# A hybrid decoder layer in float32 on one core: sums over partitions in the products' row pattern, a bias table written by Pool, and the first half's down product in plain products of 320 columns

## The chip, the cores and the metric

The kernel runs on 1 core of one Trainium2 chip, in one launch. The metric is the device time of that core in microseconds (us). The kernel before took 1602.73 us as the median of 3 runs (1602.7 to 1602.85).

## The reference

One decoder layer is computed in float32 for 320 tokens: a prompt of 256 and 8 samples of 8. The model width D is 2048.

```python
xn = rms_norm(x, g_mix)
z = xn @ w_in                      # B | C | h | q | k | v | gate_conv | gate_attn
u = c_gate * h_conv                # short causal convolution of width 3
y_conv = (b_gate * conv_out) @ w_conv_out
bias = rel_bias[t5_bucket(dist)]   # 32 buckets x 16 heads, window 128
attn = softmax_with_sink(q k^T / 8 + bias) v
y_attn = attn @ w_attn_out
h = x + (sigmoid(gate_c) * y_conv + sigmoid(gate_a) * y_attn) @ w_o
hn = rms_norm(h, g_ffn)
h = h + (silu(hn @ w_gate) * (hn @ w_up)) @ w_down     # 5632 hidden features
y = rms_norm(h, g_final)
```

Beside y, the new window of keys and values and the last rows of u are returned.

## The kernel before, in words

**Products.** Features lie on the partitions and the 320 tokens along the free axis. A float32 product is made of three products of rounded parts (type fp32r): with w = whi + wlo and x = xh + xl it is whi x xh + whi x xl + wlo x xh, all added up in PSUM. The weights are the stationary operand, 128x128 at a time, and the 320 tokens stream past. Each weight tile comes by DMA on SP's queue (wraw, 512 KB), ACT rounds it to whi (L128) and DVE subtracts to get wlo (L129); four wraw and three whi/wlo buffers let this run ahead of TensorE. `product` (L161 to L184) does one group: 2 blocks of 128 outputs, 96 products where the depth is 2048.

**Row pattern.** The 320 tokens of a chunk are stored as 5 pieces of 64 (`fives`), a fixed pitch apart, and are streamed 4 tokens of each piece in turn (`turns`), so the moving operand has the shape 16x5x4. In the built programs each such row starts 64 bytes past a multiple of 256; the leads LEAD_X, LEAD_C, LEAD_A and LEAD_M set that. A few products don't follow the pattern: the sums over partitions for the norms (`over_partitions`, L198, with a 128x128 tile of ones as weights, ones_r), the transposes and products of the attention, and a `nudge` (L194), which multiplies a plain row and throws the result away. There are four nudges.

**Order.** The stages follow one another on TensorE: kv, q, three kinds of gates and inputs (C, H, B, four rounds), the gates of the merge with the two output products (gc, ga, yc, ya, eight rounds), wo, and the feed-forward part. Attention is a generator (`side_work`) that is advanced one step after each weight tile of a running product, so its small products stand between those of q, C, H and B. A scheduler in the framework orders each engine's instructions from these; dependencies alone make an engine wait.

**First norm** (`first_norm`, L428). The squares are added up in xacc, split into two parts (`two_parts`, L186), and summed over the partitions in `prb`, between the second and the third of the four weight tiles of the first q product. Just ahead of it two small products (`pe_`, L441) multiply the bias table, 32 buckets x 16 heads, by a one-hot matrix of 32 x 128; DVE copies the result into e_sb, and Pool's queue stores it (e_scr) and loads the rows of the bias from there for the scores.

**Feed-forward part.** The 44 chunks of hidden features are done in two halves of 28 and 16. In each half, gate (fg) and up (fu) products come first, two chunks at a time, then the down product. Between the first fg and fu stands the second norm's sum (`pss`). **The down product** (`down`, L938) goes by blocks of 512 outputs with four accumulators. A chunk's hidden row holds both parts of the later 192 tokens, but only the rounded part of the first 128. So per chunk there are four products of 512 columns with whi (L962), one of 512 columns with the row's low part as weights and whi streaming (L966, into dl, or into rowacc for the last block), and four of 320 columns with wlo (L970). The low parts come out with tokens on the partitions; they are kept in ylow and added at the end. The second half's last block is taken apart and written out by hand (L1114 to L1161), and adds to the same rowacc.

Of the kernel before, what the change touches and what calls it, by code (L numbers as in the profile page):

```python
# [21 lines left out]
WIN = 128  # L22
# [29 lines left out]
def hybrid_layer(ctx: ExitStack, tc: tile.TileContext, a: dict, o: list):  # L52
# [133 lines left out]
    def two_parts(src, tags=("ta", "tb")):  # L186

        n = src.shape[-1]
        hi, lo = (wk.tile([P, UL], F32R, tag=t, name=u("part"))[:, :n] for t in tags)
        nc.scalar.activation(hi, src, AF.Copy)  # L190
        nc.vector.tensor_sub(lo, src, hi.bitcast(F32))
        return hi, lo
# [5 lines left out]
    def over_partitions(out, parts):  # L198
        for i, x in enumerate(parts):
            nc.tensor.matmul(out, ones_r, x, start=i == 0, stop=i == 1)  # L200
# [70 lines left out]
    rel = zz.tile([NBK, NH], F32, name="rel")  # L271
    oh = zz.tile([NBK, WIN], F32, name="oh")
    rel_r = zz.tile([NBK, 2, NH], F32R, name="rel_r")
    oh_r = zz.tile([NBK, WIN], F32R, name="oh_r")
# [103 lines left out]
    def small_loads():  # L378

        behind = nc.gpsimd.tensor_copy(gate, xh(7)[:, 0, 0:1].bitcast(F32))  # L380
        with after(behind):
            nc.gpsimd.dma_start(rel, a["rel_bias"])
            nc.gpsimd.dma_start(oh, a["c_onehot"])
            nc.gpsimd.dma_start(sink_bc, sk[0].partition_broadcast(P))
            nc.gpsimd.dma_start(sink_s, bass.AP(sk.tensor, sk.offset, [[1, NH], [0, TS], [1, 1]]))
            nc.gpsimd.dma_start(st_sb, a["state_t"])
            nc.gpsimd.dma_start(blk, a["c_block"])
# [40 lines left out]
    def first_norm():  # L428
# [5 lines left out]
        parts = two_parts(xacc)  # L434
        nc.vector.tensor_copy(oh_r, oh)
        nc.scalar.activation(rel_r[:, 0], rel, AF.Copy)
        nc.vector.tensor_sub(rel_r[:, 1], rel, rel_r[:, 0].bitcast(F32))
        yield
        prb, pe_ = ps_aux("prb"), ps_aux("pe_")
        for i in range(2):  # L440
            nc.tensor.matmul(pe_[:NH, :WIN], rel_r[:, i], oh_r, start=i == 0, stop=i == 1)  # L441
# [7 lines left out]
        nc.vector.tensor_copy(e_sb[:, WIN - 1:2 * WIN - 1], pe_[:NH, :WIN])  # L449
# [481 lines left out]

    def parts_of(row):
        return placed(row[:, 0:P]), placed(row[:, P:])
# [4 lines left out]
    def down(half, c0):  # L938

        nf, f0 = FH[half], half * FH[0]  # L940
        ps = [ps_acc(u("dn")) for _ in range(4)]
        low = ps_aux(u("dl")) if c0 < E0 else rowacc
        sets = [[k] for k in range(0, nf, 2)]
        sets[-2:] = [sets[-2] + sets[-1]]
        for i, k0s in enumerate(sets):
            parts = {}
            for k0 in k0s:
                raw = wp.tile([P, 2, 512], F32, tag="wraw", name=u("wraw"), bufs=4)
                nc.sync.dma_start(raw, w_d[c0 // 512, :, f0 + k0:f0 + k0 + 2, :])
                hi = wp.tile([P, 2, 512], F32R, tag="whi", name=u("whi"), bufs=3)  # L950
                lo = wp.tile([P, 2, 512], F32R, tag="wlo", name=u("wlo"), bufs=3)
                split_to(hi, lo, raw)
                for j in range(2):
                    parts[k0 + j] = (hi[:, j, :], lo[:, j, :])
            end = i == len(sets) - 1
            order = [(k, c) for k in parts for c in range(4)]
            if end or i == 0:
                order.sort(key=lambda kc: kc[1])
            for k, c, m in passes(order, end):
                cs = slice(c * P, (c + 1) * P)  # L960
                if m == 0:
                    nc.tensor.matmul(  # L962
                        turns(placed(ps[c])), parts[k][0][:, cs], turns(a_move(k)), start=k == 0, stop=False
                    )
                elif m == 1 and c == 0:
                    nc.tensor.matmul(  # L966
                        low, a_low(k), parts[k][0], start=k == 0, stop=k == nf - 1 and c0 < E0
                    )
# [15 lines left out]
        if c0 < E0:  # L984
            ys = ylow[:, c0:c0 + 512]
            if half == 0:
                nc.scalar.activation(ys, low, AF.Copy)
            else:
                nc.vector.tensor_add(ys, low, ys)

    for half in range(2):
# [3 lines left out]
        a_move, a_low, a_first, free = a_rows(half)  # L995
        for fpair in range(nf // 2):
            c0 = (f0 + fpair * 2) * P
            if half == 0 and fpair == 1:
                nudge(hh, hl, P)
# [16 lines left out]
            if half == 1 and fpair == 0:  # L1016
                nudge(hh, hl, P)
# [4 lines left out]
            for c in range(2):  # L1022
                nc.vector.tensor_mul(gs[c], psu[c][:, :T], gs[c])
                f = fpair * 2 + c
                (first, rest), row = parts_of(gs[c]), a_move(f)
# [4 lines left out]
                if half == 1:  # L1030
                    nc.scalar.activation(a_first(f), gs[c][:, 0:P], AF.Copy)
# [46 lines left out]
        for c0 in range(0, D if half == 0 else E0, 512):  # L1078
            down(half, c0)
            if half == 1:  # L1080
# [183 lines left out]
```

## Time and profile before

| what | value |
|---|---|
| median of 3 runs | 1602.73 us (1602.7 to 1602.85) |
| profiled execution, span from first to last instruction | 1600.6 us; no other time is given for it |
| TensorE busy | 1592.1 us, 10957 products |
| DVE, ACT, Pool busy | 885.6, 651.4, 78.3 us |
| granted TensorE clock, mean | 0.999 |
| data moved | 258.14 MB, 161 GB/s over the span |

The chain of waits is the work that ended last, followed back from the last instruction; shown in order of time, a line gives the start (us), the duration (us) up to what follows, the engine, the tile written, the line of the program, and the count. A timeline of one engine has the same columns, then the tiles (out<-in) and their sizes, and in brackets the idle time ahead and what ended it. In a list of DMA issues the columns are the size in KB and the time from issue to landing. Products overlap, so the duration of a single one (302 ns for 320 columns) is longer than the step from one to the next.

### The profile page before, as it was taken

The numbers are of one execution on the slowest core, as the hardware profiler recorded it, in microseconds if no ns is written. First come the engines' busy times: TensorE is split into PE (matmuls) and PEld (weight loads), VectorE is DVE, ScalarE is ACT, GpSimd is POOL, SyncE is SP. The second block draws the span as 40 slices with busy tenths as digits, with TensorE's granted clock in tenths as the row PEclk, the third lists the DMA queues.
The fourth block names the chain that finished last, engine by engine and source line by source line (L and its number), as shares of the span: only waits on it lengthen the run. The fifth ranks groups of instructions, "written<-read, shape, count | busy, mean of one in ns | idle before, by whom it ended". The sixth has DMA issues, their size and how long they took to land.

```text
span 1600.6 us, 26409 instructions
## 1 busy us (share of the span) xinstructions
PE 1592.1 (99%) x10957; PEld 1555.5 (97%) x10957; DVE 885.6 (55%) x1316; ACT 651.4 (41%) x928; POOL 78.3 (5%) x123
## 2 busy tenths in 40 slices
PE   9999999999999999999999999999999999999998
PEld 9999999999999999999999999998888999999887
DVE  7879565444455555556555555553444455555556
ACT  7555433433333334444333333333333334344443
POOL 1101311000000003320000000000000000000000
PEclk9999999999999999999999999999999999999999
DMA  7554546545444545544444445455555544545552
GB/s 276 174 170 137 182 145 200 167 158 156 154 157 157 157 157 159 158 158 155 154 157 156 157 157 159 158 158 158 155 154 155 157 156 158 158 158 157 182 175 93
DMA packets 74400, 258.14 MB, mean 161 GB/s; under 512 B 8552, under 2 KB 11928, under 8 KB 74152
## 3 DMA queue, kind: packets, MB, share of 16 engines
q1 hardware_dynamic: 71880, 249.86, 49.4%
q0 software_dynamic: 1968, 5.90, 1.3%
q8 instruction: 86, 1.41, 0.4%
q10 hardware_dynamic: 432, 0.69, 0.1%
q14 instruction: 34, 0.28, 0.1%
HBM read 253.30 MB, written 5.08 MB: 161 GB/s over the span
## 4 chain that ended last, share of the span: by engine, by line
PE 99%; DVE 0%; ACT 0%; DVEq 0%; issue 0%
PE fu L175 18%; PE fg L175 18%; PE dn L962 9%; PE gc L175 7%; PE ga L175 7%; PE wo L175 7%; PE dn L970 6%; PE B L175 3%; PE C L175 3%; PE H L175 3%; PE q L175 3%; PE yc L175 3%; PE ya L175 3%; PE dl L966 2%; PE kv L366 2%; PE dn L1114 1%
## 5 line engine op out<-in xcount | busy, mean ns | idle before, releaser
L129 DVE TENSOR_TENSOR wlo<-wraw,whi 128x1024 fp32r<-128x1024 f32 (+1 forms) x460 | 561.7, 1221 | 588.7 <-ACT whi L128 580.5
L128 ACT ACTIVATE whi<-wraw 128x1024 fp32r<-128x1024 f32 (+1 forms) x460 | 485.0, 1056 | 717.3 <-PE dn L962 144.7
L962 PE MATMUL dn<-a_t,whi 128*128 128x512 f32 x640 | 211.1, 385 | 0.0
L175 PE MATMUL fu<-hh_t,whi 128*128 128x320 f32 x704 | 205.3, 302 | 0.0
L175 PE MATMUL fg<-hl_t,whi 128*128 128x320 f32 x704 | 205.3, 302 | 0.0
L175 PE MATMUL fu<-hl_t,whi 128*128 128x320 f32 x704 | 205.3, 302 | 0.0
L175 PE MATMUL fg<-hh_t,whi 128*128 128x320 f32 x704 | 205.3, 302 | 0.0
L175 PE MATMUL fg<-hh_t,wlo 128*128 128x320 f32 x704 | 159.0, 302 | 0.0
L175 PE MATMUL fu<-hh_t,wlo 128*128 128x320 f32 x704 | 159.0, 302 | 0.0
L970 PE MATMUL dn<-a_t,wlo 128*128 128x320 f32 x640 | 146.8, 302 | 0.0
L962 PEld LDWEIGHTS dn<-a_t,whi 128*128 128x128 f32 x640 | 118.8, 188 | 19.3
L175 PEld LDWEIGHTS fg<-hh_t,whi 128*128 128x128 f32 x704 | 131.9, 187 | 0.0
L175 PEld LDWEIGHTS fu<-hh_t,whi 128*128 128x128 f32 x704 | 131.9, 187 | 0.0
L175 PEld LDWEIGHTS fg<-hl_t,whi 128*128 128x128 f32 x704 | 131.8, 187 | 0.0
L175 PEld LDWEIGHTS fu<-hl_t,whi 128*128 128x128 f32 x704 | 131.8, 187 | 0.0
L970 PEld LDWEIGHTS dn<-a_t,wlo 128*128 128x128 f32 x640 | 111.2, 188 | 9.3
L175 PEld LDWEIGHTS fu<-hh_t,wlo 128*128 128x128 f32 x704 | 116.3, 187 | 0.0
L175 PEld LDWEIGHTS fg<-hh_t,wlo 128*128 128x128 f32 x704 | 116.3, 187 | 0.0
L175 PE MATMUL ga<-xl_t,whi 128*128 128x320 f32 x256 | 74.6, 301 | 0.0
L175 PE MATMUL gc<-xl_t,whi 128*128 128x320 f32 x256 | 74.6, 302 | 0.0
L175 PE MATMUL wo<-m_l,whi 128*128 128x320 f32 x256 | 74.6, 302 | 0.0
L175 PE MATMUL gc<-xh_t,whi 128*128 128x320 f32 x256 | 74.6, 301 | 0.0
(313 smaller groups left out, 2681.4 us busy)
## 6 DMA issues: line engine op xcount, KB each, us to landing
wraw<-in_w_in_dram SPq DMA_DIRECT2D x128, 512.0 KB, 3.8
wraw<-in_w_gate_dram SPq DMA_DIRECT2D x88, 512.0 KB, 3.8
wraw<-in_w_up_dram SPq DMA_DIRECT2D x88, 512.0 KB, 3.7
wraw<-in_w_down_dram SPq DMA_DIRECT2D x88, 512.0 KB, 3.6
wraw<-in_w_o_dram SPq DMA_DIRECT2D x32, 512.0 KB, 3.7
wraw<-in_w_conv_out_dram SPq DMA_DIRECT2D x16, 512.0 KB, 3.6
wraw<-in_w_attn_out_dram SPq DMA_DIRECT2D x16, 512.0 KB, 3.6
wraw<-in_w_kv_dram SPq DMA_DIRECT2D x6, 512.0 KB, 7.4
```

Of the source, the lines that this page charges most:

```text
L128: last["hi"] = nc.scalar.activation(hi, src, AF.Copy)
L129: last["lo"] = nc.vector.tensor_sub(lo, src, hi.bitcast(F32))
L175: last["mm"] = nc.tensor.matmul(turns(fives(ps[c][:, :T])), w[:, k, c * P:(c + 1) * P], turns(x(kc)), start=(kc == 0 and i == 0), stop=(kc ...
L366: last["mm"] = nc.tensor.matmul(turns(fives(ps[c][:, :T])), w[:, k, c * P:(c + 1) * P], turns(x(kc)), start=(kc == 0 and m == 0), stop=(kc ...
L962: nc.tensor.matmul(turns(placed(ps[c])), parts[k][0][:, cs], turns(a_move(k)), start=k == 0, stop=False)
L966: nc.tensor.matmul(low, a_low(k), parts[k][0], start=k == 0, stop=k == nf - 1 and c0 < E0)
L970: last["mm"] = nc.tensor.matmul(turns(placed(ps[c])[:, :, 0:JT]), parts[k][1][:, cs], turns(a_move(k)[:, :, 0:JT]), start=False, stop=k == ...
L1114: nc.tensor.matmul(turns(placed(ps[c])[:, :, JR:]), held[k][0][:, cs], turns(a_move(k)[:, :, JR:]), start=k == 0, stop=k == nf - 1,)
```

## The change

There are three edits, and what follows from them.

1. The norms' sums over partitions. `two_parts` becomes `two_rows`: the two parts are written as rows of an existing row tile (at_t's chunk 7 in the first norm, the new hidden rows' chunk 27 in the second) and `over_partitions` streams them with `turns`, as the products do. The two nudges in the feed-forward part go; the two ahead of it stay.
2. The bias table. The one-hot matrix, its load and its product go. The table is loaded transposed (relT, 16 heads x 32 buckets), one element at a time, and Pool writes e_sb by 17 copies: the first 16 distances have a bucket each, and each of the other 16 buckets is spread over its run of distances.
3. The first half's down product. The hidden rows of the first half are now kept like all other rows, with both parts for all 320 tokens (`a_fives`, a pitch of 1808 elements), and `down_first` makes three products of 320 columns for each chunk and each of the four accumulators. DVE adds 320 columns at once to the result. ylow is then written in the second half alone, by a copy on ACT where DVE added before, and rowacc starts in the second half.

```diff
-    def two_parts(src, tags=("ta", "tb")):
-        n = src.shape[-1]
-        hi, lo = (wk.tile([P, UL], F32R, tag=t, name=u("part"))[:, :n] for t in tags)
-        nc.scalar.activation(hi, src, AF.Copy)
-        nc.vector.tensor_sub(lo, src, hi.bitcast(F32))
+    def two_rows(src, hi, lo):
+        nc.scalar.activation(hi, fives(src), AF.Copy)
+        nc.vector.tensor_sub(lo, fives(src), hi.bitcast(F32))
         return hi, lo
...
         for i, x in enumerate(parts):
-            nc.tensor.matmul(out, ones_r, x, start=i == 0, stop=i == 1)
+            nc.tensor.matmul(turns(fives(out)), ones_r, turns(x), start=i == 0, stop=i == 1)
...
-            nc.gpsimd.dma_start(rel, a["rel_bias"])
-            nc.gpsimd.dma_start(oh, a["c_onehot"])
+            nc.gpsimd.dma_start(relT, a["rel_bias"].rearrange("b h -> h b"))
...
-        parts = two_parts(xacc)
-        nc.vector.tensor_copy(oh_r, oh)
-        nc.scalar.activation(rel_r[:, 0], rel, AF.Copy)
-        nc.vector.tensor_sub(rel_r[:, 1], rel, rel_r[:, 0].bitcast(F32))
-        yield
-        prb, pe_ = ps_aux("prb"), ps_aux("pe_")
-        for i in range(2):
-            nc.tensor.matmul(pe_[:NH, :WIN], rel_r[:, i], oh_r, start=i == 0, stop=i == 1)
+        parts = two_rows(xacc, at_h(7), at_l(7))
+        at, one_each = [_bucket(c) for c in range(WIN)], NBK // 2
+        nc.gpsimd.tensor_copy(e_sb[:, WIN - 1:WIN - 1 + one_each], relT[:, :one_each])
+        for b in range(one_each, NBK):
+            c, n = WIN - 1 + at.index(b), at.count(b)
+            nc.gpsimd.tensor_copy(e_sb[:, c:c + n], relT[:, b:b + 1].to_broadcast([NH, n]))
+        yield
+        prb = ps_aux("prb")
...
-        nc.vector.tensor_copy(e_sb[:, WIN - 1:2 * WIN - 1], pe_[:NH, :WIN])
...
+    def a_fives():
+        step = FH[0] * JS + 16
+        part = -(-NS * step // JS) * JS
+        flat = fp.tile([P, LEAD_F + A_ALL], F32R, tag="at", name=u("a_t"))
+        return [rows_in(flat, LEAD_C + i * part, step, lambda k: k * JS) for i in range(2)]
...
+    def down_first(c0):
+        nf = FH[0]
+        ps = [ps_acc(u("dn")) for _ in range(4)]
+        sets = sets_of(nf)
+        for i, ks in enumerate(sets):
+            parts = {}
+            for k in ks[::2]:
+                parts |= down_weights(0, c0, k)
             end = i == len(sets) - 1
+            order = [(k, c) for k in ks for c in range(4)]
+            if end or i == 0:
+                order.sort(key=lambda kc: kc[1])
+            for k, c, m in passes(order, end):
+                w, x = ((0, a_hi), (0, a_lo), (1, a_hi))[m]
+                last["mm"] = nc.tensor.matmul(
+                    turns(fives(ps[c][:, :T])), parts[k][w][:, c * P:(c + 1) * P], turns(x(k)),
+                    start=k == 0 and m == 0, stop=k == nf - 1 and m == 2,
+                )
+        for c in range(4):
+            k = c0 // P + c
+            nc.vector.tensor_add(hT[:, k, :], ps[c][:, :T], hT[:, k, :])
...
-        if c0 < E0:
-            ys = ylow[:, c0:c0 + 512]
-            if half == 0:
-                nc.scalar.activation(ys, low, AF.Copy)
-            else:
-                nc.vector.tensor_add(ys, low, ys)
+        nc.scalar.activation(ylow[:, c0:c0 + 512], low, AF.Copy)
...
-            if half == 0 and fpair == 1:
-                nudge(hh, hl, P)
...
-                over_partitions(pss[:, :T], two_parts(hacc, ("tc", "td")))
+                over_partitions(pss[:, :T], two_rows(hacc, a_hi(FH[0] - 1), a_lo(FH[0] - 1)))
...
-            if half == 1 and fpair == 0:
-                nudge(hh, hl, P)
...
+                if half == 0:
+                    split_to(a_hi(f), a_lo(f), fives(gs[c]))
+                    continue
...
-            last["mm"] = nc.tensor.matmul(rowacc, x, wh, start=False, stop=k == nf - 1 and m == 1)
+            last["mm"] = nc.tensor.matmul(rowacc, x, wh, start=k == m == 0, stop=k == nf - 1 and m == 1)
```

`down_weights` holds the load and the split of one weight tile, as they stood in `down` before; `sets_of` takes the chunks in twos, the last four together. `down` keeps its old products for the second half.

How the instructions stand on TensorE's queue at the first norm, behind the second weight tile of the first q product; q_504 and q_505 (q_500 and q_501 in the change) are its two accumulators, and the last column is the moving operand's shape. Before:

```order
L175 MATMUL q_504<-xh_t,wlo_561 128x16x5x4
L175 MATMUL q_505<-xh_t,wlo_561 128x16x5x4
L441 MATMUL pe__589<-oh_r,rel_r 16x128 x2
L200 MATMUL prb<-part_551,ones_r 128x320
L200 MATMUL prb<-part_552,ones_r 128x320
L175 MATMUL q_504<-xh_t,whi_614 128x16x5x4
```

Now:

```order
L175 MATMUL q_500<-xh_t,wlo_569 128x16x5x4
L175 MATMUL q_501<-xh_t,wlo_569 128x16x5x4
L198 MATMUL prb<-at_t,ones_r 128x16x5x4 x2
L175 MATMUL q_500<-xh_t,whi_618 128x16x5x4
L175 MATMUL q_500<-xl_t,whi_618 128x16x5x4
```

The place is the same; the two table products are gone, and the two sums have the products' shape.

On TensorE's queue in the first block of the down product, its third chunk (a_t are the hidden rows, dn the four accumulators, dl the low part). Before:

```order
L962 MATMUL dn_11267<-a_t_7524,whi_11298 128x16x8x4
L966 MATMUL dl_11271<-whi_11298,a_t_7524 128x512
L962 MATMUL dn_11268<-a_t_7524,whi_11298 128x16x8x4
L962 MATMUL dn_11269<-a_t_7524,whi_11298 128x16x8x4
L962 MATMUL dn_11270<-a_t_7524,whi_11298 128x16x8x4
L970 MATMUL dn_11267<-a_t_7524,wlo_11299 128x10x8x4
```

Now:

```order
L968 MATMUL dn_11211<-a_t_7528,whi_11247 128x16x5x4 x2
L968 MATMUL dn_11212<-a_t_7528,whi_11247 128x16x5x4 x2
L968 MATMUL dn_11213<-a_t_7528,whi_11247 128x16x5x4 x2
L968 MATMUL dn_11214<-a_t_7528,whi_11247 128x16x5x4 x2
L968 MATMUL dn_11211<-a_t_7528,wlo_11248 128x16x5x4
```

Each accumulator takes two products of 320 columns with whi in place of one of 512, and the products that stream the weights are gone; those with wlo stay where they were, 16x5x4 in place of 10x8x4.

On Pool's queue at the table. Before:

```order
L382 DMA rel<-in_rel_bias_dram 32x16
L383 DMA oh<-in_c_onehot_dram 32x128
L384 DMA sink_bc<-in_sinks_dram 128x16
L385 DMA sink_s<-in_sinks_dram 128x1x1
L386 DMA st_sb<-in_state_t_dram 128x128
L387 DMA blk<-in_c_block_dram 64x8
L450 DMA e_scr<-e_sb 16x384
L802 MEMSET ue_1524 128x2
L803 COPY ue_1524<-st_sb 128x8x2
L451 DMA bias_s<-e_scr 128x1x136
```

Now:

```order
L377 DMA relT<-in_rel_bias_dram 16x32x1
L378 DMA sink_bc<-in_sinks_dram 128x16
L379 DMA sink_s<-in_sinks_dram 128x1x1
L380 DMA st_sb<-in_state_t_dram 128x128
L381 DMA blk<-in_c_block_dram 64x8
L430 COPY e_sb<-relT 16x16
L433 COPY e_sb<-relT 16x3
L433 COPY e_sb<-relT 16x2
L433 COPY e_sb<-relT 16x3 x2
...
L443 DMA e_scr<-e_sb 16x384
L444 DMA bias_s<-e_scr 128x1x136
```

The load of the table stands ahead of the sinks' loads as before; the copies (9 more rows at the dots) stand behind all small loads and ahead of the store of the bias rows.

More of the change, by code (lines that the diff above doesn't have):

```diff
@@ L957, in down @@
+    def down(c0):
+        nf = FH[1]
+        ps = [ps_acc(u("dn")) for _ in range(4)]
+        low = ps_aux(u("dl"))
+        sets = sets_of(nf)
+        for i, ks in enumerate(sets):
+            parts = {}
+            for k in ks[::2]:
+                parts |= down_weights(1, c0, k)
+            end = i == len(sets) - 1
+            order = [(k, c) for k in ks for c in range(4)]
             if end or i == 0:
@@ L966, in down @@
                     nc.tensor.matmul(
-                        low, a_low(k), parts[k][0], start=k == 0, stop=k == nf - 1 and c0 < E0
+                        low, a_low(k), parts[k][0], start=k == 0, stop=k == nf - 1
                     )
@@ L1248 @@
     arrays, args, outs = {}, {}, []
[L1249 removed]
+    for name, v in [(n, inputs[n]) for n in _INS] + [("c_block", block)]:
         v = _np.ascontiguousarray(v)
```

50 lines of the change are left out of this document (22 added, 28 removed).

## The prediction, made before the changed kernel ran

> **What bounds the kernel now.** I read the page first, then the chain of waits in order of time, then the timelines of single engines where an edit touches them.
>
> ```profile
> span 1600.6 us, 26409 instructions
> PE 1592.1 (99%) x10957; PEld 1555.5 (97%) x10957; DVE 885.6 (55%) x1316; ACT 651.4 (41%) x928; POOL 78.3 (5%) x123
> PE 99%; DVE 0%; ACT 0%; DVEq 0%; issue 0%
> ```
>
> TensorE is busy for 1592.1 of 1600.6 us and is 99% of the chain. The other engines wait for it. So only three things can move the end: how many columns TensorE streams, how fast it streams them, and whether a new wait opens. The chain in order of time gives the rate (start, duration, what):
>
> ```profile
> 15.56 16.80 PE kv L366 x120
> ...
> 298.41 6.72 PE yc L175 x48
> 305.13 6.72 PE ya L175 x48
> ...
> 594.09 107.52 PE wo L175 x768
> ```
>
> 6.72 us for 48 products, 16.80 for 120 and 107.52 for 768 are all 140.0 ns for a product of 320 columns; 96 of them make 13.44. The rate holds across changes of tile (xh, cv_h, at_t, m_h), and with four accumulators (kv) as with two. But there is a second rate:
>
> ```profile
> 715.05 0.30 PE pss L200 x2
> 715.35 13.66 PE fu L175 x96
> 729.01 0.06 PE nudge L196
> 729.07 13.49 PE fg L175 x96
> ```
> ```profile
> 1267.12 13.66 PE fg L175 x96
> 1280.78 0.06 PE nudge L196
> 1280.84 13.49 PE fu L175 x96
> ```
>
> After two products that read their rows plainly (pss), the next 96 take 13.66 us, 142.3 ns each. They are not slow only at the start, since 96 of them lose 0.22 us and the 96 after the nudge are back at 13.49. The same happens behind the first half's down product. I call these the fast and the slow step, 140.0 and 142.3 ns.
>
> **The change part by part.** *Second norm.* From pss to the end of the second product the rows give 0.30 + 13.66 + 0.06 + 13.49 = 27.51 us. Changed, the two sums stream 320 columns in the products' own pattern, 2 x 0.14, the nudge is gone, and if the fast step survives the two products take 26.88: 27.16. That is **-0.35 us**. *Behind the down product*: 13.66 + 0.06 + 13.49 = 27.21 becomes 26.88, **-0.33 us**, on the same condition.
>
> *The first half's down product.* It has 28 chunks of the hidden features times 4 blocks. Before, a chunk took four products of 512 columns, one of 512 for the low part and four of 320: 3840 columns in 9 instructions. Now it takes twelve of 320: 3840 columns in 12 instructions. So the columns do not change, and the question is the price of an instruction.
>
> ```profile
> 1065.12 13.44 PE fu L175 x96
> 1082.38 0.67 PE dn L962 x3
> 1085.74 0.67 PE dn L962 x3
> ```
>
> Two chunks repeat after 1085.74 - 1082.38 = 3.36 us, 1.68 us a chunk. Twelve products at 140.0 ns are 1.68 us too. So in the steady part nothing changes: 512 columns in this pattern cost 1.6 times 320, and three more instructions cost nothing of their own. The whole stage runs from 1065.12 + 13.44 = 1078.56 to 1267.12, where fg begins above, 188.56 us; 112 chunks at 1.68 are 188.16. The 0.40 us between them lies where the pattern breaks off at the ends of the blocks, and uniform products have no such place (kv, four accumulators, 120 products, exactly 16.80). I take all of it, **-0.40 us**; the bounds are 0 and -0.40.
>
> The Trainium skill, "TensorE: Matmul & The Clock Gate", section "Back-to-back issue gap", would have it otherwise: the columns over 2.4 GHz plus about 2.5 ns for every matmul. By that rule, three more instructions a chunk cost 7.5 ns, 0.8 us over 112 chunks, and the whole change would gain 0.3 us. The trace disagrees: the measured chunk of nine and twelve measured products both take 1.68 us, and the measurement decides.
>
> *First norm.*
>
> ```profile
> 32.36 6.72 PE q L175 x48
> 39.08 0.22 PE pe__589 L441 x2
> 39.30 0.48 PE prb L200 x2
> 39.78 10.10 PE q L175 x72
> 49.88 0.22 PE pk L493 x2
> ...
> 91.47 0.24 PE ps L542 x2
> ```
>
> From 32.36 to 49.88 are 17.52 us. The two table products (0.22) go. The two sums fall from 0.48 to 0.28, if part of the 0.48 is the switch from the table's 32-row weights, which also go. With 120 products at 140.0 the piece takes 16.80 + 0.28 = 17.08: **-0.44 us**; if the sums keep their 0.48, -0.24.
>
> *The table on Pool and its load.* The one-hot load and two small rounding steps on ACT and DVE go. In their place come one load of the table, element by element (16 x 32), and 17 copies on Pool, ahead of the store and the loads of the bias rows on Pool's own queue.
>
> ```profile
> 14.63 0.57 POOL L384 DMA_DIRECT2D sink_bc<-in_sinks_dram  x1
> 15.19 0.55 POOL L385 DMA_DIRECT2D sink_s<-in_sinks_dram  x1
> ```
> ```profile
> L803 POOL COPY ue<-st_sb x8: 190/386/1227, 40.5 to 221.2; 128x16 f32<-128x16 f32 x8
> ```
> ```profile
> sink_bc<-in_sinks_dram POOLq DMA_DIRECT2D x1, 8.0 KB, 6.2
> sink_s<-in_sinks_dram POOLq DMA_DIRECT2D x1, 0.5 KB, 6.5
> ```
>
> No load of 512 elements is in the trace. The nearest is sink_s, 128 elements of 4 bytes, 0.55 us to issue and 6.5 us to land, no worse than its neighbours. Below it costs 0.55 us on Pool, above four times that, 2.2 us. What is queued behind it is sink_bc, for which DVE waits at nsink; the copies take 17 x 0.39 = 6.6 us by the median of the nearest copy (190, 386 and 1227 ns are its shortest, median and longest: 3.2 and 21 us at the ends) from about 29 us, when e_sb is cleared.
>
> ```profile
> 28.70 0.17 DVE L431 TENSOR_SCALAR nsink<-sink_bc 128x16 f32<-128x16 f32 x1
> 28.88 0.38 DVE L433 MEMSET e_sb<- 16x384 f32 x1
> 31.77 0.49 DVE L191 TENSOR_TENSOR part<-xacc,part 128x320 fp32r<-128x320 f32 x1
> 36.34 1.23 DVE L129 TENSOR_TENSOR wlo<-wraw,whi 128x1024 fp32r<-128x1024 f32 x1 [1.85 <-ACT whi L128]
> ```
>
> sink_bc lands near 14.63 + 6.2 = 20.8, DVE wants it at 28.70, so 7.9 us cover a delay of 2.2. The sums are ready at 31.77 + 0.49 = 32.26 and used at 39.08, and DVE idles 1.85 us for ACT ahead of a later split; copies that hold DVE up would come out of those. The bias rows are first needed by the scores, whose first products stand at 91.47 in the chain; even 21 us of copies let the bias rows go out at 50. So **0**, hidden under the q products. In the Trainium skill, "DMA: Bandwidth & Descriptors", section "Rules for kernel authors", stands that a strided last dimension becomes one descriptor per element and is to be rearranged. It speaks against this load, and sink_s, the same kind a quarter of the size, bears no sign of a price.
>
> *Splits and sums of the first half* need fewer instructions on ACT and DVE (1 and 1 for 2 and 2, one addition of 320 columns for three), under a TensorE that they do not hold up now: 0. *In the second half* the low part is now copied by ACT, not added by DVE. At the last block this stands ahead of a weight split:
>
> ```profile
> 1558.87 1.06 ACT L128 ACTIVATE more<-wraw 128x1024 fp32r<-128x1024 f32 x1 [0.29 <-DMA wraw<-in_w_down_dram]
> 1560.77 1.06 ACT L128 ACTIVATE whi<-wraw 128x1024 fp32r<-128x1024 f32 x1 [0.84 <-DMA wraw<-in_w_down_dram]
> ```
> ```profile
> 1120.74 0.60 ACT L987 ACTIVATE ylow<-dl 128x512 f32<-128x512 f32 x1 [1.31 <-PE dl L966]
> ```
>
> The copy of 0.60 us fits into the 0.84 us in which ACT waits for a load: 0. Without that cover it would be 0.6 us on a split.
>
> *The attention stage* keeps its order, but the narrower tiles move its operands by 64 bytes, and there the step changes with nearly every insertion:
>
> ```profile
> 118.78 3.42 PE B L175 x24
> ...
> 167.77 3.42 PE B L175 x24
> ...
> 192.93 7.03 PE C L175 x48
> 199.96 10.24 PE H L175 x72
> ```
>
> Five pieces of 24 read 3.41 or 3.42 (first and last shown), and with the 48 and 72 some 240 of the 864 products in this stage (nine groups of 96) take the slow step. Bounds: all fast -0.5 us, all slow 624 x 2.3 ns = +1.4. I take 0, since nothing says which way.
>
> Sum: -0.35 - 0.33 - 0.40 - 0.44 = -1.52 us on a span of 1600.6. The median of the runs is 2.1 us above that span, the start and end around it, which the change does not touch: 1602.73 - 1.52 = **1601.2**. A measurement of this kernel can tell about 0.2%, 3.2 us, from no change, so this is no change.
>
> **Rivals.** *The slow step stays (slower).* The condition of two terms is that sums with ones_r as weights leave the step fast. In the built program the new rows start at the same offset as every product's row (64 bytes past a multiple of 256), and crossings between such rows kept 140.0. For the rival: ones_r itself lies at another offset, pss used it and was followed by the slow step, and no nudge is left to mend it. Against: prb used it too and the 72 products behind took 10.10, 140.3 each. If it decides, 27 groups of 96 in the first half pay 0.22 each (5.9 us), the down product 1344 x 2.3 ns (3.1) and the second half's 16 groups 3.5: 1601.2 + 12.5 = **1613.7**; if the down product ends it, 1607.1. Chance 9%.
>
> *The down product does not stream as it says.* Its rows lie 1808 elements apart, a pitch no row has shown (1040, 528 and 144 did). With the slow step there it costs 3.1 us, **1604.3**, and 1607.8 if it carries into the second half. For it: a new layout; against: three pitches with one rate. Chance 6%.
>
> *The element-wise load holds up DVE.* It decides from 7.9 us of delay on, each us beyond costing at most one; a delay of 11 us would give **1604.3** at most. Against: 128 elements cost 0.55 us. Chance 2%.
>
> *Faster than forecast.* With the attention stage all fast and the whole sum met: **1600.7**. More than 0.2% faster has no mechanism in these rows; 3% for what they don't show.
>
> **How the numbers follow.** My forecast, -0.9 to -2.0 us with the attention stage near where it is, has 70%; the attention stage worse, up to +1.4, or a first norm at its smaller gain, 10% (1602.0 to 1602.9). The range goes from 1600.5 (all bounds at their best, 1600.7, and the spread of runs) to 1603.3 (attention all slow, 1602.6, no gain at the first norm and at the blocks' ends). It leaves out the rivals above it. Slower by over 0.2%, beyond 1605.9: the first rival and half of the second, 12%; faster, below 1599.5: 3%; within: 85%.
>
> **What would show it.** Right: fu behind pss at 13.44, no piece of 13.66 behind the down product, four blocks in 188.2 us, prb at 0.28 with q directly around it, and the first DVE row that reads sink_bc still near 28.7. Wrong: pieces of 13.66 in a row from 715 us on, or a down product of 191 us, or an idle TensorE near 36 us with Pool or a load as its releaser.

## The result, and the profile after

The changed kernel takes 1611.55 us as the median of 6 runs, against 1602.72 us for the kernel before on the same chip: a ratio of 1.0066, with a 95% interval of 1.0055 to 1.0076. It is slower, by 8.8 us. Its runs fall into two groups, four at 1611.0 to 1611.7 us and two at 1617.2 and 1617.5; those of before lie between 1602.5 and 1602.9. The profiled execution took 1611.41 us with a span of 1609.7, 9.1 us more than before.

The head of the page of the changed kernel:

```profile
span 1609.7 us, 26984 instructions
PE 1599.8 (99%) x11289; PEld 1583.6 (98%) x11289; DVE 874.8 (54%) x1250; ACT 649.4 (40%) x899; POOL 83.4 (5%) x139
```

TensorE is still the bound, and busy for 7.7 us more, although it streams fewer columns. The other 1.4 us of the span are time in which it stands still. So look for a slower rate and for a gap. The timeline of TensorE, at the places where the prediction's chain had them (start, duration, what; a product of 320 columns is 0.30 us long but the next starts 0.14 behind it):

```profile
32.70 0.30 PE L175 MATMUL q<-xh_t,whi 128*128 128x320 f32 x1
49.79 0.38 PE L486 MATMUL pk<-ident,vT 128*128 128x128 f32 x2
...
600.18 0.30 PE L175 MATMUL wo<-m_h,whi 128*128 128x320 f32 x1
709.41 0.30 PE L175 MATMUL fg<-hh_t,whi 128*128 128x320 f32 x1
723.06 0.44 PE L198 MATMUL pss<-a_t,ones_r 128*128 128x320 f32 x2
723.34 0.30 PE L175 MATMUL fu<-hh_t,whi 128*128 128x320 f32 x1
736.78 0.30 PE L175 MATMUL fg<-hh_t,whi 128*128 128x320 f32 x1
```

From the first q product to pk, the piece with the first norm, are 49.79 - 32.70 = 17.09 us, where the prediction had 17.08. But the 768 products of wo take 709.41 - 600.18 = 109.23 us, 142.2 ns each; before they took 107.52. The first fg behind them takes 13.65. Then come the two sums (pss), and fu behind them is back at 736.78 - 723.34 = 13.44. So the slow step now stands where it never stood for long before, in the 500 us ahead of the second norm, and ends at the very sums after which it used to begin.

The second place is the start of the down product. The timelines of ACT, DVE and TensorE there (in brackets the idle time ahead and what ended it):

```profile
1085.66 0.72 PE L175 MATMUL fu<-hh_t,wlo 128*128 128x320 f32 x4
1085.91 1.06 ACT L128 ACTIVATE whi<-wraw 128x1024 fp32r<-128x1024 f32 x1 [0.17 <-PE fu L175]
1086.94 0.47 ACT L128 ACTIVATE a_t<-gs 128x320 fp32r<-128x320 f32 x1
1087.47 0.83 PE L968 MATMUL dn<-a_t,whi 128*128 128x320 f32 x4 [1.08 <-ACT a_t L128]
1088.14 0.48 DVE L129 TENSOR_TENSOR a_t<-gs,a_t 128x320 fp32r<-128x320 f32 x1
1088.68 1.12 PE L968 MATMUL dn<-a_t,whi 128*128 128x320 f32 x6 [0.38 <-DVE a_t L129]
1276.40 0.30 PE L175 MATMUL fg<-hh_t,whi 128*128 128x320 f32 x1
```

The last product of fu starts at 1085.66 + 3 x 0.14 and the next could at 1086.22. It starts at 1087.47, when ACT has written the rounded part of the last hidden chunk (behind the split of a weight tile), and after four products TensorE waits again until DVE has written the low part at 1088.62. Yet these first products read chunks 0 and 1, written some 350 us earlier. From 1086.22 to the second half's first fg at 1276.40 are 190.18 us, of which 1344 products at 140.0 ns are 188.16: this wait, the stall in what follows, costs **2.0 us**. The rest of the stage streams as forecast, and nothing slow follows (chain of waits in order of time):

```profile
1088.68 187.88 PE dn L968 x1340
1276.56 13.44 PE fg L175 x96
```

The whole difference of the two profiled executions, from these rows and those that the prediction quotes:

| stretch | before, us | after, us | difference |
|---|---|---|---|
| up to the first q product (timelines: 32.20 and 32.70) | | | +0.5 |
| first q product to pk | 17.52 | 17.09 | -0.4 |
| pk to the first wo product | 544.21 | 550.39 | +6.2 |
| wo | 107.52 | 109.23 | +1.7 |
| fg ahead of the second norm | 13.44 | 13.65 | +0.2 |
| sums and the two products behind | 27.51 | 27.16 | -0.35 |
| end of the last fu to the second half's fg | 188.56 | 190.18 | +1.6 (stall +2.0, block ends -0.4) |
| the two products behind the down product | 27.21 | 26.88 | -0.33 |
| sum | | | +9.1 |

The first row is no part of the change: two kernels of the experiments (e_down and e_shift), which are the kernel before up to that point, have their first q product at 32.52 and 32.44, and the changed kernel itself has it at 32.52 in its second profile (experiment 8).

### The profile page after: what moved, and what is told of

Its sections match the earlier page's. It is cut to its first block, busy times and chain, and to the rows that moved or that the text cites. A ratio compares the mean times of both kernels' runs of the same rounds, so it can differ in the third digit from the quotient of the medians.

```text
span 1609.7 us, 26984 instructions
## 1 busy us (share of the span) xinstructions
PE 1599.8 (99%) x11289; PEld 1583.6 (98%) x11289; DVE 874.8 (54%) x1250; ACT 649.4 (40%) x899; POOL 83.4 (5%) x139
## 5 line engine op out<-in xcount | busy, mean ns | idle before, releaser
L968 PE MATMUL dn<-a_t,whi 128*128 128x320 f32 x896 | 163.0, 301 | 1.5 <-ACT a_t L128 1.1
L968 PEld LDWEIGHTS dn<-a_t,whi 128*128 128x128 f32 x896 | 137.5, 187 | 2.0 <-ACT a_t L128 1.3
L968 PE MATMUL dn<-a_t,wlo 128*128 128x320 f32 x448 | 103.9, 301 | 0.0
L175 PE MATMUL wo<-m_h,whi 128*128 128x320 f32 x256 | 75.3, 303 | 0.0
```

The costliest lines, as they stand in the source:

```text
L175: last["mm"] = nc.tensor.matmul(turns(fives(ps[c][:, :T])), w[:, k, c * P:(c + 1) * P], turns(x(kc)), start=(kc == 0 and i == 0), stop=(kc ...
L968: last["mm"] = nc.tensor.matmul(turns(fives(ps[c][:, :T])), parts[k][w][:, c * P:(c + 1) * P], turns(x(k)), start=k == 0 and m == 0, stop= ...
```

## The experiments

Each kernel ran beside the kernel before, which took 1602.9 to 1603.1 us in these comparisons. In the built programs attention's tiles lie 32 bytes past a multiple of 256 in the kernel before (s_s, the scores of the sample part, named for all) and 96 in the changed one: the tiles that the change removed and added in the pool ahead of them sum to 1088 bytes less, which is 4 x 256 + 64. Where 64 bytes are spoken of below, this place modulo 256 is meant.

**1. The changed kernel with attention's tiles put back by 64 bytes** (e_pad).

```diff
-    relT = zz.tile([NH, NBK], F32, name="relT")
+    relT = zz.tile([NH, NBK + 16], F32, name="relT")[:, :NBK]
```

> The changed kernel with one edit: relT is 48 columns wide instead of 32 (the last 16 are never used), so that every tile that attention allocates behind it lies 64 bytes lower and has the place modulo 256 bytes that it had in the kernel before. No instruction is added or removed. Theory O (offsets): the place of the operands of the sample part's transposes decides which of the two product steps they leave behind, and that step lasts until the second norm. It expects the products from 211 to 723 us at 140.0 ns instead of 142.2, which is 512 x (1 - 140.0/142.2) = 7.9 us less: 1603.5 us, and no run near 1617, since with the fast step ahead of the second norm it no longer matters whether its sums change the step. Rival T (timing): the slow step comes from what the new order of Pool, DMA and sums does to the moments at which attention's pieces run. It expects 1611.4 and the runs near 1617 unchanged.

**2. The kernel before with attention's tiles moved by 64 bytes** (e_shift).

```diff
-    rel = zz.tile([NBK, NH], F32, name="rel")
+    rel = zz.tile([NBK, NH + 48], F32, name="rel")[:, :NH]
```

The 48 columns are 192 bytes; they put s_s at 96, its place in the changed kernel.

> The kernel before with one edit: rel is 64 columns wide instead of 16 (the last 48 are never used), which moves attention's tiles to the place modulo 256 bytes that they have in the changed kernel. Nothing of the change itself is in it. Theory O expects the slow step from 211 us until the kernel's own reset behind the second norm's sums at 730 us: 519 x (1 - 140.0/142.2) = 8.0 us more, 1610.7 us, in one mode, since that reset is still there. Rival T expects 1602.7.

**3. The changed kernel with the hidden rows in two groups** (e_groups). The tile that holds them also gets 128 columns more, to have room.

```diff
-        step = FH[0] * JS + 16
+        per = FH[0] // 2
+        step = per * JS + 16
...
-        return [rows_in(flat, LEAD_C + i * part, step, lambda k: k * JS) for i in range(2)]
+        both = [[rows_in(flat, LEAD_C + (2 * g + i) * part, step, lambda k: k % per * JS) for g in range(2)] for i in range(2)]
+        return [lambda k, rows=rows: rows[k // per](k) for rows in both]
```

> The changed kernel with one edit: the first half's hidden rows lie in two groups of 14 chunks each (pitch 912 instead of 1808) instead of one of 28, so that the address range from the first to the last piece of chunk 0 no longer holds chunk 27. Instructions and their order are the same. Theory R (range): the first products of the down product wait for the split of chunk 27 because the ranges of interleaved rows overlap. It expects the stall of 2.0 us at 1087 us gone and the rest the same: 1609.4 us where the changed kernel has 1611.4, and 1615.4 where it has 1617.4. Rival W (weights): the products wait for the split of their own weights, which now stands behind the hidden rows' splits on ACT and DVE; it expects the stall unchanged, 1611.4. Should the pitch of 912 stream worse than 1808, the down product's 1344 products would say so with a mean above 140.0 ns.

**4. Both edits, 1 and 3** (e_padgroups).

> The two edits together: relT 48 columns wide, and the hidden rows of the first half in two groups. Theories O and R expect the sum of both gains, 1611.4 - 7.9 - 2.0 = 1601.5 us, in one mode, which is 1.2 us under the kernel before: what the prediction had worked out (1601.2). T with R expects 1609.4, O with W 1603.5.

Measured: e_pad 1609.74 us (four runs of 1609.1 to 1609.8, one of 1615.33; ratio 1.0048, interval 1.0035 to 1.0060), e_shift 1616.01 (1.0080, 1.0067 to 1.0094), e_groups 1609.11 (1.0039, 1.0023 to 1.0054), e_padgroups 1614.13 (1.0068, 1.0056 to 1.0081).

Experiment 3 did what theory R said: 2.4 us less than the changed kernel, four runs within 0.8 us of each other (one mode), and no product waits for a_t. Its chain of waits runs through the place without a gap:

```profile
218.88 1.99 PE spo L720 x64
...
231.31 13.65 PE C L175 x96
...
599.95 109.23 PE wo L175 x768
...
722.82 0.28 PE pss L198 x2
723.11 13.44 PE fu L175 x96
...
1085.98 188.16 PE dn L970 x1344
```

This chain also shows what that of the changed kernel, which breaks off at the stall, does not: behind the sample part's products (spo) every product is at 142.2 ns, through C, wo and fg, until the sums.

Theory O was right on attention and wrong on what follows. In experiment 4, and in 1 likewise, wo is fast, as O expected, but now the sums leave the slow step (chain of e_padgroups):

```profile
595.08 107.52 PE wo L175 x768
...
716.04 0.28 PE pss L198 x2
716.33 13.65 PE fu L175 x96
...
1084.96 191.15 PE dn L970 x1344
1276.11 13.65 PE fg L175 x96
```

The slow step then lasts over 27 groups (27 x 0.213 = 5.8 us) and, in experiment 4, through the down product and the second half as well (1344 x 0.0022 + 16 x 0.213 = 6.4). In experiment 1 the stall ended it. The gain of 7.9 us ahead of the norm was lost again behind it. And the kernel before, with nothing changed but the place of attention's tiles (chain of e_shift):

```profile
600.50 109.23 PE wo L175 x768
...
723.37 0.30 PE pss L200 x2
723.67 13.45 PE fu L175 x96
737.12 0.06 PE nudge L196
737.18 13.71 PE fg L175 x96
```

Here the old sums, in their plain pattern, found the slow step and left the fast one behind, and the nudge that ends the slow step in the kernel before began it, up to the down product at 1092 us. That is 7.8 us ahead of the sums and 26 x 0.213 = 5.5 behind them, less the 0.2 of the one group that was slow in the kernel before: 13.1 us, against 12.9 between the medians. Theory T is out as the cause: the other place alone, with nothing of the change, cost more than the change did.

So I formed theory S, that the sums and the single products turn the step over (fast behind slow, slow behind fast), and set against it O2, that what they leave behind doesn't depend on what they find.

**5. Edits 1 and 3 with the single product ahead of the second gate product kept** (e_best).

```diff
+            if half == 0 and fpair == 1:
+                nudge(hh, hl, P)
```

> The two edits of the last run but one (relT 48 wide; hidden rows in two groups) and a third: the single product nudge(hh, hl, P) ahead of the second gate product, where the kernel before had it. Theory S (state): the step is a state that each break in the row of equal products can change; the second norm's two sums leave the state other than they found it (slow behind fast, fast behind slow), whatever pattern they read, and what follows keeps it until the next break. It expects 140.0 ns from 211 to 716 us, 142.2 for the one product group of 13.65 us behind the sums, and 140.0 from the nudge to the end of the second half's up products: 1614.1 - 26 x 0.213 (groups to 1086) - 1344 x 0.0022 - 16 x 0.213 (down product and second half) = 1602.2 us, or from the kernel with the groups alone 1609.1 - 7.9 + 0.3 = 1601.5; 1601.8 taken, 0.1% under the kernel before. Rival N: the nudge does not act on this state behind turned sums; 1614.1.

**6. The changed kernel with a single product behind attention** (e_nudge).

```diff
+        if cp == 3:
+            nudge(xh, xl, T)
         ps = in_pair(O_C + cp * CW, "C")
```

> The changed kernel, its widths and offsets untouched, with one product nudge(xh, xl, T) ahead of the last C product (231.5 us), behind the sample part of attention. Theory S expects 140.0 ns from there to the second norm, 491.5 x (1 - 140.0/142.2) = 7.6 us less, and then the sums to leave the slow step behind, since they now find the fast one: 27 x 0.213 = 5.8 us more, up to the stall at 1086 us, which leaves the fast step: 1611.4 - 7.6 + 5.8 + 0.1 = 1609.7 us. Rival O2: what the sums leave is decided by the offsets of their operands and not by what they find; with the changed kernel's offsets they leave the fast step: 1603.9.

**7. Edit 3 with both single products** (e_nudges).

> The hidden rows in two groups and both single products (ahead of the last C product and ahead of the second gate product), with relT as the change has it. Theory S expects the fast step from 231.5 us on but for one group behind the sums: 1609.1 - 7.6 + 0.1 + 0.2 + 0.1 = 1601.9 us, 0.3 above the padded version, whose attention leaves the slow step 20 us earlier (20 x 0.0156 = 0.3). Rival O2 expects the second nudge to turn the fast step into the slow one as it did in the shifted kernel before (737 to 1092 us): 1601.5 + 5.6 + 6.4 = 1613.5.

**8. The changed kernel again** (e_again).

> The changed kernel once more, unedited, for one look. Theory S: its two times, 1611.4 and 1617.4, differ in what the stall of 2 us at 1086 us leaves behind. Where the profile is one of the slower ones, the products are at 140.0 ns from 723 to 1086 us and at 142.2 from 1089 us to the end of the second half's up products (1344 x 0.0022 + 16 x 0.213 = 6.4 us). Rival: the sums at 723 us do not leave the slow step in those runs, 142.2 ns from 723 to 1086 us (5.8 us) and 140.0 behind.

Measured: e_best 1601.89 us (11 runs, 1601.4 to 1602.2; ratio 0.9994, interval 0.9985 to 1.0003), e_nudge 1604.33 (six runs of 1604.0 to 1604.6, four of 1610.1 to 1610.8; 1.0023, 1.0011 to 1.0035), e_nudges 1613.75 (1.0068, 1.0054 to 1.0082), e_again 1611.46.

Experiments 6 and 7 came out as O2 had them (1603.9 and 1613.5), so theory S falls for the sums: they find the fast step now, and the products behind them are still fast. The same nudge that helps in experiment 5 harms in 7 (chain of e_nudges, then of e_best); it turned the step over in both:

```profile
231.49 0.15 PE nudge L194
231.63 13.44 PE C L175 x96
...
715.76 13.44 PE fu L175 x96
729.20 0.06 PE nudge L194
729.26 13.71 PE fg L175 x96
```
```profile
594.28 107.52 PE wo L175 x768
...
715.52 13.65 PE fu L175 x96
729.17 0.06 PE nudge L194
729.23 13.50 PE fg L175 x96
```

Experiment 8 gave the lower of the two times and so settles nothing on the higher one. It shows something else: the same kernel came out otherwise at the first norm. In the first profile the 72 q products behind the sums prb take 49.79 - 39.71 = 10.08 us, in this one 49.76 - 39.52 = 10.24, with the products ahead at 140.0 ns in both (timeline of the first profile, then of e_again):

```profile
39.71 0.30 PE L175 MATMUL q<-xh_t,whi 128*128 128x320 f32 x1
```
```profile
39.52 0.30 PE L175 MATMUL q<-xh_t,whi 128*128 128x320 f32 x1
49.76 0.38 PE L486 MATMUL pk<-ident,vT 128*128 128x128 f32 x2
```

The profile of experiment 6 happened to be one of its slower runs (1610.46 us), and it shows what theory S expected of those: the products are fast up to the stall, and slow behind it (chain of e_nudge):

```profile
1081.32 190.84 PE dn L970 x1340
1272.16 13.65 PE fg L175 x96
```

The same 1340 products took 187.88 us in the changed kernel's profile, so each takes 2.2 ns more here.

**9. Edit 3 with the single product behind attention alone** (e_gnudge).

> The changed kernel with the hidden rows in two groups and the single product nudge(xh, xl, T) ahead of the last C product; none behind the second norm's sums. By the two runs with that product the sums then leave the fast step. Theory: 140.0 ns from 231.5 us to the end, no stall at 1086 us and so nothing that could leave a slow step there: 1604.0 - 2.3 (what the groups alone took off) = 1601.7 us in one mode. Rival: the change of the rows' pitch, and not the stall alone, bears on the second time near 1610; then some runs lie 6.4 us higher.

**10. The kernel before with the table part of the change alone** (e_table). Its sums and down product are those of before; relT is 48 columns wide, so that attention's tiles keep their places.

> The kernel before with the table part of the change alone (17 copies on Pool in place of the two products with the one-hot array), relT 48 columns wide so that attention's tiles keep their places. The prediction has the table at 0 and its two products as a part of the first norm's 0.44: about 0.22 us less, 1602.5 (same within what can be measured). Rival: the copies or the element-wise load delay what attention needs, up to the 1604.3 that the prediction gave for it.

**11. The kernel before with the down product alone** (e_down), its rows in two groups as in edit 3.

> The kernel before with the down product of the first half as the change has it, but its rows in two groups, and without the single product ahead of the second half's first up product; the norms, their sums, the table and the widths are untouched. The prediction's terms for it: the down product -0.40, the products behind it -0.33: 1602.9 - 0.7 = 1602.2 us. Rival: the plain products' own step comes out at 142.2 (1344 x 0.0022 = 3.0 us more, and 3.4 more in the second half), 1608.6.

**12. The changed kernel with the sample part's first tiles alone moved back** (e_smpad).

```diff
-        pn = sm.tile([P, NB, TS], F32, name="pnew")
+        pn = sm.tile([P, NB * TS + 16], F32, name="pnew")[:, :NB * TS].rearrange("p (b t) -> p b t", b=NB)
```

> The changed kernel with pnew 16 columns wider (never used): of attention's tiles only kf, s_s, pnew and the cached values cv go back to their places modulo 256 bytes of the kernel before; vn, qs, kT, ptn, ptw and all tiles of the prompt part stay where the change put them. Theory A: what the sample's transposes leave at 211 us is decided by these four tiles: 140.0 ns from 211 us on. Rival B: by the places of the others, or by what the prompt part left behind: 142.2 as in the changed kernel. If A holds, the sums at 716 us tell whether the same four tiles decide what is left there (slow step as in the padded kernel, about 1609.7 us) or the others (fast step, about 1603.9); with B 1611.4.

Measured: e_gnudge 1602.06 us (11 runs, 1601.3 to 1602.2; ratio 0.9993, interval 0.9985 to 1.0002), e_table 1602.64 (0.9998, 0.9989 to 1.0007), e_down 1602.26 (0.9995, 0.9986 to 1.0005), e_smpad 1612.25 as the median of 1608.70, 1609.22, 1615.28 and 1615.54 (ratio 1.0057, interval 1.0040 to 1.0075).

Experiment 9 has one mode at the expected time. In experiment 10 the piece from the first q product to pk takes 49.64 - 32.53 = 17.11 us by its timeline, with the sums still in their plain pattern. So the gain at the first norm came with the table's two products; the row pattern added nothing to it. Experiment 11 gives the two terms at the down product by themselves (its chain):

```profile
1079.20 188.16 PE dn L977 x1344
1267.36 13.44 PE fg L175 x96
```

188.16 us is 1344 times 140.0 ns exactly, with no loss at the blocks' ends, and the products behind it are fast.

In experiment 12 theory A holds. With kf, s_s, pnew and cv back at their places the step is 140.0 ns from 211 us on, so among the tiles of attention these four decide what the transposes leave behind; the sums leave the slow step behind, as in experiment 1 (timeline of e_smpad: wo takes 701.57 - 594.05 = 107.52, fu 728.95 - 715.29 = 13.66):

```profile
594.05 0.30 PE L175 MATMUL wo<-m_h,whi 128*128 128x320 f32 x1
701.57 0.30 PE L175 MATMUL fg<-hh_t,whi 128*128 128x320 f32 x1
715.29 0.30 PE L175 MATMUL fu<-hh_t,whi 128*128 128x320 f32 x1
728.95 0.30 PE L175 MATMUL fg<-hh_t,whi 128*128 128x320 f32 x1
```

Its profile, too, was one of the slower runs (1615.54 us), and there the stall did not end the slow step: its 1340 products of dn take 190.85 us.

## Why the prediction was wrong, step by step

The forecast was 1601.2 us, no change; the kernel takes 1611.55.

**The attention stage: the step that failed most.** The prediction saw that the tiles move by 64 bytes and that the step changes with nearly every insertion there. It bounded the effect by the stage's own products, -0.5 to +1.4 us. But a step outlasts its stage: nothing between the sample part's last products and the second norm ends it, so what attention leaves behind is paid on all 3,530 products up to 723 us, 2.2 ns each or 7.8 us. The rows for seeing it stood in the prediction itself: wo, yc and ya at 140.0 ns were read as a rate that "holds across changes of tile", when they were one inheritance from attention. The bound should have been 1.4 + 7.8.

**Splits and sums of the first half, 0: failed by 2.0 us.** The instructions were counted, and not which writes a read must wait for. The five pieces of a chunk lie 1808 elements apart, so from the first to the last piece of chunk 0 the range holds pieces of all the other chunks, and the first read of chunk 0 waits for the last write of chunk 27. In the kernel before the rows lay in two groups of 14, and the last group was still being written, up to 1080.88 us, while the first was read from 1078.40 on. Experiment 3 takes the overlap away and with it the stall; that the wait is set by the range as a whole is inferred from this and from which write it waits for.

**Second norm, -0.35, and behind the down product, -0.33: right in size, for a wrong reason.** Both came in. The reason given was that rows in the products' pattern leave the step as it is. They don't: over the kernels the sums in that pattern turned slow to fast, fast to slow, or left fast alone, and the plain sums did both of the first two. In the changed kernel the slow step from attention was ended there by luck, and the term came in with it. Behind the down product the plain products do leave the fast step as they find it (experiment 11), but they leave the slow one too (experiment 4).

**First norm, -0.44: met in one profile, and there by luck.** 17.09 us against 17.08; but in experiment 8, the same kernel, it is 49.76 - 32.52 = 17.24, -0.28, near the prediction's smaller gain. Experiment 10 gets 17.11 with the table's part alone. Sums in the products' rows left the slow step behind here in six of the ten profiles that have them; the plain sums left the fast one in all four.

**The first half's down product, -0.40: right.** 188.16 us by experiment 11, which as a whole gained 0.6 us where the two terms say 0.7. Three more instructions in a chunk cost nothing, as the prediction read from the rows. By the formula in the Trainium skill ("TensorE: Matmul & The Clock Gate", section "Back-to-back issue gap") these 112 chunks would, as an estimate, have taken 0.8 us more; the section gives it for an isolated matmul and says itself that it counts too much in a stream of large ones.

**The table on Pool and its load, 0: right.** The timeline of Pool in the changed kernel and its list of DMA issues:

```profile
13.80 0.83 POOL L377 DMA_DIRECT2D relT<-in_rel_bias_dram  x1
29.75 0.34 POOL L430 COPY e_sb<-relT 16x16 f32<-16x16 f32 x1 [12.96 <-DVE e_sb L427]
30.04 4.05 POOL L433 COPY e_sb<-relT 16x3 f32<-16x3 f32 x16
34.38 0.52 POOL L443 DMA_DIRECT2D e_scr<-e_sb  x1 [0.29 <-POOL e_sb L433]
...
relT<-in_rel_bias_dram POOLq DMA_DIRECT2D x1, 2.0 KB, 6.6
```

The element-wise load took 0.83 us to issue and 6.6 to land, inside the bounds of 0.55 and 2.2 for the issue; the 17 copies took 4.3 us, not 6.6, and the bias rows could go out 57 us before the scores. DVE first reads sink_bc at 29.14 us, 0.4 after the 28.70 of before and within the 0.5 by which this profile starts its products later. The strided load that the Trainium skill warns of ("DMA: Bandwidth & Descriptors", section "Rules for kernel authors") costs 0.3 us of issue against its neighbours, and hides.

**The ACT copy of the low part, 0: right**; from the second half's first fg (1276.56 against 1267.12, 9.4 us late) to the end of the span (9.1 us late) the kernel gains the 0.33 us forecast and loses nothing.

**The rivals.** "The slow step stays" had about the right price for a case that did not come. It said the sums would leave the slow step for good, 1613.7 us; experiment 4 is that case, at 1614.1. In that case attention left the fast step behind, which it does not in the changed kernel. No rival put the slow step ahead of the second norm. "The down product does not stream as it says" is out: its pitch of 1808 streams at 140.0. The range ended at 1603.3 because it rested on the bound that failed (its own terms, 1602.6 and neither gain, add up to 1603.4).

With both faults mended the change does about what the sum said: experiment 5 takes 1601.89 us and experiment 9 1602.06, 1.1 and 0.8 us under the kernel before, where the prediction had 1.5. Both are the fastest versions that ran; their intervals reach to 1.0003 and 1.0002, so they can't be told from the kernel before.

## What to carry to other kernels

A change of tile sizes is a change of addresses for every tile allocated beside them; when the profile shows a second rate that some products take on and others lose, look for the last thing that sets it and bound the effect by all work up to the next thing that can reset it, not by the stage that is moved. Where rows are interleaved at a pitch, ask of the first read of the first row which write is the last in its whole range. A repair of a rate (a throw-away product) holds for what it finds: the same line gained where the products ahead of it were slow and lost 5.5 us or more where they were fast.

## What the runs showed that was not expected

A row of equal products of 320 columns runs at 140.0 or at 142.2 ns (96 of them in 13.44 or 13.65 us), at a granted clock of 0.998 to 0.999 in kernels with either, and keeps its step over more than 3,500 products. In these profiles only a break, other products in between or a stall, changes it. At 211 us (the sample part's transposes), at the second norm's sums and at the single product behind them, the profiles of all kernels that ran showed this:

| place of s_s, modulo 256 bytes | transposes, 211 us | second norm's sums | single product, 729 to 737 us |
|---|---|---|---|
| 32: before, e_table, e_down, e_best | slow to fast | fast to slow | slow to fast |
| 32: e_pad, e_padgroups, e_smpad | slow to fast | fast to slow | none there |
| 96: e_shift | slow, stays | slow to fast | fast to slow |
| 96: after, e_again, e_groups | slow, stays | slow to fast | none there |
| 96: e_nudge, e_gnudge (fast from 231 us on) | slow, stays | fast, stays | none there |
| 96: e_nudges (fast from 231 us on) | slow, stays | fast, stays | fast to slow |

All fourteen find the slow step at the transposes, and what these leave behind goes with the place of the sample part's tiles; experiments 1, 2 and 12 moved attention's tiles, the last only four of them, and nothing else. At the other two places the table doesn't prove as much. The single product of 128 columns turned the step over every time, so that the place and the step it finds can't be told apart there; in experiment 2 one began the slow step at 737 us and the next, at 1294, ended it (13.66 us ahead, 13.49 behind) with the tiles at the same place. The sums turned it over too, except in the three profiles with the single product at 231 us. There the fast step came from that product and not from the transposes, and this is a rival to the place that no run separates from it. Nor can the place be all: at the first norm the two profiles of the changed kernel, with the same places, came out fast and slow. What sets the outcome of a break 500 us after attention is open.

A stall of 2 us is a break of another kind: what it leaves differs from run to run. The four kernels that have it and ran several times all have two times 6 us or so apart (2 of 6 runs of the changed kernel, 1 of 5 of e_pad, 4 of 10 of e_nudge and 2 of 4 of e_smpad are the later one); the nine others, the kernel before among them, have one. Two profiles of the later kind show the slow step behind the stall, from either step ahead of it, and three of the earlier kind show the fast one, which is worth 6.4 us up to the end of the second half's up products. No kernel has a profile of both kinds, and the changed kernel has none of the later; that its two later runs were slow behind the stall is inferred. If so, a wait of 2 us cost it 2 us at best and some 8 in a third of its runs.
